# Lengths by products with a column of ones, a k scaled once, 32 decay columns and five sums side by side in a two-layer trunk

## The chip, the core and the metric

The kernel runs on one core of a Trainium2 chip. A core has a matrix engine (TensorE, PE in the profile, with its weight loads shown apart as PEld), a vector engine (VectorE, DVE), an activation engine (ScalarE, ACT), GpSimd (POOL) and SyncE (SP), which issues most of the DMAs. Each engine takes its own queue in order; they wait for each other by semaphores. The metric is the device time of one execution in microseconds, less is better.

## The reference

The reference is a decoder trunk of two layers over 528 positions (16 learned ones and 512 of the input) with 1024 channels, in float32. Layer 0 mixes positions with a chunked gated DeltaNet, layer 1 with a short gated convolution; each mixer is followed by a gated feed-forward with a convolution (2816 channels), and each sub-layer ends in a LayerNorm of 1.41 x + f(x).

The DeltaNet has 8 heads of 128 channels. q, k and v come from a projection, a causal convolution of four taps and a Silu. What the change touches is this:

```python
def l2norm(x):
    return x * lax.rsqrt(jnp.sum(x * x, axis=-1, keepdims=True) + L2_EPS)
...
    q = l2norm(q) * (GDN_HEAD_DIM ** -0.5)
    k = l2norm(k)
    beta = jax.nn.sigmoid(b_raw)
    g = -jnp.exp(a_log) * jax.nn.softplus(a_raw + dt_bias)
...
    decay = jnp.exp(jnp.where(causal, g[..., :, None] - g[..., None, :], -jnp.inf))
    k_beta = k * beta[..., None]
    v_beta = v * beta[..., None]
    m = jnp.where(strict, jnp.einsum("bhnid,bhnjd->bhnij", k_beta, k) * decay, 0.0)
    a_mat = jnp.eye(CHUNK) + m
    u = triangular_solve(a_mat, v_beta);  w = triangular_solve(a_mat, k_beta * exp(g))
```

Here g is the running sum within a chunk; the state then passes through the chunks one after the other.

## The kernel before

Activations lie with channels on the 128 partitions and positions along the free dimension. Every large product is done in three matmuls: an operand is split into a high part (hi, rounded to fp32r by ScalarE) and the rest (lo, by VectorE), and hi*hi, hi*lo and lo*hi are summed in PSUM (lines 286 to 288, `mm_steps`). Weights are loaded in strips of 128 output channels, split by `split` (lines 91 and 92) and used strip by strip; `pump` loads and splits ahead as far as buffers go.

**The recurrence** (lines 345 to 693) takes the 528 positions as five chunks of 106. First come the decay and beta columns: 16 columns of weights, two halves of the positions (tile psba, lines 347 to 350), transposed to positions on partitions (psb), and a series of small operations on 106 x 40 values. `proj` projects k, v and q of a head, in this order, convolves them and applies Silu. `gdn_a` prepares a head: it transposes k and v (pk, pv), forms the products of k with k (pn) and with q (pp), takes lengths from squares of the transposed k and q (lines 473 and 474, 499 to 502), scales the matrix by beta and the lengths (psNb, lines 506 to 510), and inverts it by levels of masked f16 products. `gdn_b` runs the state through the five chunks, `gdn_c` transposes the output back, and `gate` projects z. The matrix of decays of a head (`decay`, tile psE) is made for two heads at a time, both in the PSUM tile ga0; `gdn_a` of even heads uses ga0, of odd heads ga1, one step after another in the same tile.

The generators of three heads are woven (lines 673 to 686), and the projection of a later head follows in program order. The order in which each engine gets its instructions is set by a planner, when the kernel is built: it takes ready instructions by priority, which is program order, and by its own estimates of durations. So projections fill PE between the small steps of the recurrence. On the chip the order is fixed, and an engine that waits holds up all that is planned behind.

**The sub-layers.** `down` multiplies a group of hidden blocks (gh, gl, nk blocks of 128) with the down strips into tiles pd, one sum for each output strip m and half b of the positions, and adds them to h (line 773 for the first group, 775 for later ones). `together` runs several sums side by side, block after block, so that a block that arrives late is needed later. At the start of a group three sums run so. PSUM has six banks for this (tag m) and two others (tag a), which the LayerNorm uses. The out projection is `down` with nk = 8, the first feed-forward uses nk = 4, 6, 6, 6, the short convolution 2 and 6; the last feed-forward has its own function, `down_turned`.

Of the kernel before, what the change touches and what calls it, by code (L numbers as in the profile page):

```python
# [17 lines left out]
P = 128  # L18
# [58 lines left out]
def tile_hybrid_trunk(ctx, tc, xt, par, cst, msk, w_ba, w_qkv, w_z, w_ao, w_bi, w_bo, w_up, w_dn, w_dt, lnr, out):  # L77
# [23 lines left out]
    ba_hi = lnp.tile([P, KD, 16], F32R, name="ba_hi", tag="c", bufs=CB)  # L101
    ba_lo = lnp.tile([P, KD, 16], F32R, name="ba_lo", tag="c", bufs=CB)
# [189 lines left out]
    split(ba_hi, ba_lo, ba_raw)  # L292
# [34 lines left out]
    with ExitStack() as gctx:  # L327
# [17 lines left out]
        ba_sb = gp.tile([16, TP], F32, name="ba_sb", tag="ba_sb")  # L345
        V.memset(ba_sb[:, T:], 0.0)
        psba = gtile("psba", 1).rearrange("p (b c) i -> p b (c i)", b=2)
        for b in range(2):
            mm(psba[:16, b, :HB], (ba_hi, ba_lo), KD, hh, hl, 0, b * HB, HB)
            S.activation(ba_sb[:, b * HB : (b + 1) * HB], psba[:16, b, :HB], AF.Copy)  # L350
        psb = gtile("psb")
        for c in range(NC_):
            TE.transpose(psb[:CH, c, :16], ba_sb[:, c * CH : (c + 1) * CH], ident[:16, :16])
        colb = gp.tile([CH, NH, NC_], F32, name="colb", tag="colb")
        cola = gp.tile([CH, NH, NC_], F32, name="cola", tag="cola")
        S.activation(colb, psb[:CH, :NC_, 0:8].rearrange("p c h -> p h c"), AF.Exp, scale=-1.0)
# [40 lines left out]
        nbeg = cpool.tile([CH, NH, NC_], F32, name="nbeg")  # L397
# [4 lines left out]
        V.tensor_tensor(nbeg, nb, eg, ALU.mult)  # L402

        def decay(hd):
            PT = PTs[hd] = gp.tile([CH, NC_, CH], F32, name=f"PT{hd}", tag="PT", bufs=4)
            ps = outer(gA[:, hd, :], gA_hi[:, hd, :], gA_lo[:, hd, :], tri, f"E{hd}", 0, G)
            S.activation(PT, ps[:CH, :NC_, :CH], AF.Exp)
            G.tensor_tensor(PT, PT, bcm(tri, NC_), ALU.mult)

        def proj(hd, res):  # L410
# [4 lines left out]
            for grp in (1, 2, 0):  # L415
# [15 lines left out]
                S.activation(res[grp][:, :T], acc, AF.Silu)  # L431
            if hd % 2 == 0:
# [23 lines left out]
        def gdn_a(hd, box, qT, kT, vT):  # L456
# [5 lines left out]
            ssk, ssq, rk, nbr, nbe = (small(x) for x in ("ssk", "ssq", "rk", "nbr", "nbe"))  # L462
# [5 lines left out]
            box.update(PT=PT, DT=DT, kd=kd, vb=vb, ssq=ssq, nbe=nbe, rk=rk, qT=qTv, kT=kTv)  # L468

            ps = gtile(f"pk{hd}", ch)  # L470
            for c in R5:
                TE.transpose(ps[:CH, c, :], kTv[:, c, :], ident)
            S.activation(kd, ps[:CH, :NC_, :], AF.Square)
            V.reduce_sum(ssk, kd, axis=AX)
            V.tensor_scalar(ssk, ssk, L2_EPS, None, ALU.add)
            G.tensor_tensor(rk, ssk, halfneg[:CH], ALU.pow)
            V.tensor_tensor(kd, ps[:CH, :NC_, :], bc(ekd[:, hd, :], P), ALU.mult)
# [4 lines left out]
            V.tensor_tensor(vb, ps[:CH, :NC_, :], bc(beta[:, hd, :], P), ALU.mult)  # L482
# [11 lines left out]
            V.tensor_tensor(nbr, rk, nb[:, hd, :], ALU.mult)  # L494
            G.tensor_tensor(NT, NT, bc(rk, CH), ALU.mult)
            yield 900, 1200
            ps = gtile(f"pq{hd}", ch)
            for c in R5:
                TE.transpose(ps[:CH, c, :], qTv[:, c, :], ident)
            sq = gp.tile([CH, NC_, P], F32, name=f"sq{hd}", tag="R", bufs=2)  # L500
            S.activation(sq, ps[:CH, :NC_, :], AF.Square)
            V.reduce_sum(ssq, sq, axis=AX)
            V.tensor_tensor(nbe, nbr, eg[:, hd, :], ALU.mult)
            yield 500, 15000
# [729 lines left out]
```

## Time and profile before

| what | value |
|---|---|
| runs | 1322.82, 1324.2, 1325.62 us (median 1324.2) |
| profiled execution | 1323.19 us, of which the span shown is 1321.2 us |
| granted clock of PE, mean | 0.997 |
| busy: PE, PEld | 1295.1 us (98%), 1244.6 us (94%) |
| busy: DVE, ACT, POOL | 1062.2 us (80%), 739.8 us (56%), 90.1 us (7%) |
| decay columns and recurrence | 0 to about 366 us |
| first feed-forward, its first down projection | from 464 us |
| short convolution, its first down projection | 836 to 849 us |

A matmul's span in the profile is longer than the time that it holds up PE: matmuls overlap, so the time from one start to the next is its cost in a dense stream. An f32 matmul that is not a transpose shows as two instructions. A row of the timeline gives start, length, engine, line, tiles, shapes and count, with the idle time before it and what ended it in brackets. A group row gives count, busy time, mean length in ns, and the idle time before it.

### The profile page before, as it was taken

The page shows a single profiled execution, that of the slowest core. Times are in us where ns is not written, and L with a number is a line of the kernel's source. Part 1 is how long each engine was busy: PE and PEld are TensorE (multiplying, and loading weights), DVE is VectorE, ACT ScalarE, POOL GpSimd, SP SyncE. Part 2 cuts the span into 40 slices and gives each one's busy share as a digit, 9 for nine tenths or more (in the row PEclk, how much of TensorE's full clock was granted, in tenths as well). Part 3 has the DMA queues.
Part 4 walks back from the last instruction along what each step waited for, and adds up shares of the span by engine and source line. Part 5 has one row for each costly group of instructions (what it writes and reads, how often), then busy time and mean ns, then how long its engine had stood idle before and what let it go on. Part 6 is the DMA issues. An engine that isn't in the chain of part 4 may idle for free.

```text
span 1321.2 us, 25891 instructions
## 1 busy us (share of the span) xinstructions
PE 1295.1 (98%) x10545; PEld 1244.6 (94%) x10545; DVE 1062.2 (80%) x1906; ACT 739.8 (56%) x1371; POOL 90.1 (7%) x132
## 2 busy tenths in 40 slices
PE   9999999999999999999999999999999999999997
PEld 8899989999899999999999999999998998998996
DVE  6787878786468888969869789988689795995977
ACT  6567576665345746636537467455476572662660
POOL 0323242211010000000000000000000000000000
PEclk9999999999999999999999999999999999999999
DMA  6211111111261132412422422324033242341231
GB/s 202 79 49 34 47 35 49 49 34 33 65 225 50 52 124 85 140 65 88 152 65 86 139 71 65 107 96 159 18 99 110 74 138 76 97 149 46 97 125 64
DMA packets 36183, 116.81 MB, mean 88 GB/s; under 512 B 4192, under 2 KB 5600, under 8 KB 36064
## 3 DMA queue, kind: packets, MB, share of 16 engines
q1 hardware_dynamic: 35280, 112.77, 27.0%
q0 software_dynamic: 640, 2.12, 0.5%
q8 instruction: 82, 1.34, 0.4%
q14 instruction: 37, 0.30, 0.1%
q10 hardware_dynamic: 144, 0.26, 0.1%
HBM read 113.05 MB, written 2.10 MB: 87 GB/s over the span
## 4 chain that ended last, share of the span: by engine, by line
PE 67%; DVE 5%; ACT 2%; DMA 1%; issue 1%; POOL 0%; DVEq 0%; ACTq 0%; POOLq 0%
PE px L286 6%; PE px L288 6%; PE px L287 6%; PE pd L286 5%; PE pd L287 5%; PE pd L288 5%; PE pz L286 3%; PE pz L287 3%; PE pt L841 3%; PE pt L842 3%; PE pt L843 3%; PE pz L288 3%; PE pu L287 2%; PE pu L288 2%; PE pu L286 2%; PE pq L286 2%
## 5 line engine op out<-in xcount | busy, mean ns | idle before, releaser
L91 ACT ACTIVATE wh<-raw 128x512 fp32r<-128x512 f32 (+3 forms) x309 | 234.7, 766 | 194.3 <-PE pd L287 62.4
L92 DVE TENSOR_TENSOR wl<-raw,wh 128x512 fp32r<-128x512 f32 (+3 forms) x309 | 262.6, 860 | 60.5 <-ACT wh L91 58.6
L286 PE MATMUL pd<-gh,wh 128*128 128x260 f32 (+2 forms) x480 | 135.9, 285 | 2.4 <-ACT gh L91 1.8
L91 ACT ACTIVATE wh<-s 128x512 fp32r<-128x512 f32 x129 | 81.2, 630 | 100.4 <-PE pt L842 45.3
L287 PE MATMUL pd<-gl,wh 128*128 128x260 f32 (+2 forms) x480 | 136.4, 285 | 0.3 <-DVE gl L92 0.3
L288 PE MATMUL pd<-gh,wl 128*128 128x260 f32 (+2 forms) x480 | 135.8, 283 | 0.0
L287 PE MATMUL pu<-hl,wh 128*128 128x258 f32 (+3 forms) x400 | 114.4, 289 | 1.5 <-DVE hl L754 1.4
L286 PE MATMUL pu<-hh,wh 128*128 128x258 f32 (+3 forms) x400 | 113.2, 288 | 0.7 <-ACT wh L91 0.7
L288 PE MATMUL pu<-hh,wl 128*128 128x258 f32 (+3 forms) x400 | 113.4, 288 | 0.5 <-DVE wl L92 0.5
L286 PE MATMUL ps<-hh,wh 128*128 128x264 f32 x384 | 113.5, 296 | 0.3 <-ACT acc L425 0.3
L288 PE MATMUL ps<-hh,wl 128*128 128x264 f32 x384 | 113.7, 297 | 0.0
L287 PE MATMUL ps<-hl,wh 128*128 128x264 f32 x384 | 113.2, 295 | 0.0
L92 DVE TENSOR_TENSOR wl<-s,wh 128x512 fp32r<-128x512 f32 x129 | 88.5, 686 | 12.7 <-ACT wh L91 10.6
L286 PE MATMUL px<-sumh,wh 128*128 128x258 f32 (+1 forms) x344 | 97.6, 284 | 0.0
L288 PE MATMUL px<-sumh,wl 128*128 128x258 f32 (+1 forms) x344 | 97.5, 283 | 0.0
L287 PE MATMUL px<-suml,wh 128*128 128x258 f32 (+1 forms) x344 | 97.3, 283 | 0.0
L286 PE MATMUL px<-hh,wh 128*128 128x258 f32 (+1 forms) x344 | 97.2, 283 | 0.0
L288 PE MATMUL px<-hh,wl 128*128 128x258 f32 (+1 forms) x344 | 96.9, 282 | 0.0
L287 PE MATMUL px<-hl,wh 128*128 128x258 f32 (+1 forms) x344 | 96.9, 282 | 0.0
L286 PEld LDWEIGHTS pd<-gh,wh 128*128 128x128 f32 x480 | 90.5, 189 | 3.1 <-ACT gh L91 2.0
L287 PEld LDWEIGHTS pd<-gl,wh 128*128 128x128 f32 x480 | 91.4, 191 | 0.7 <-DVE gl L92 0.5
L288 PEld LDWEIGHTS pd<-gh,wl 128*128 128x128 f32 x480 | 91.4, 191 | 0.0
(319 smaller groups left out, 4069.0 us busy)
## 6 DMA issues: line engine op xcount, KB each, us to landing
raw<-in_w_up_dram SPq DMA_DIRECT2D x88, 512.0 KB, 3.7
raw<-in_w_bi_dram SPq DMA_DIRECT2D x24, 512.0 KB, 3.7
raw<-in_w_qkv_dram SPq DMA_DIRECT2D x23, 512.0 KB, 3.6
raw<-in_w_dt_dram SPq DMA_DIRECT2D x22, 512.0 KB, 4.4
raw<-in_w_dn_dram SPq DMA_DIRECT2D x24, 384.0 KB, 3.5
raw<-in_w_z_dram SPq DMA_DIRECT2D x8, 512.0 KB, 3.6
raw<-in_w_ao_dram SPq DMA_DIRECT2D x8, 512.0 KB, 3.6
raw<-in_w_bo_dram SPq DMA_DIRECT2D x8, 384.0 KB, 3.5
```

The source lines that it names most:

```text
L91: S.activation(hi, src, AF.Copy)
L92: V.tensor_tensor(lo, src, hi.bitcast(F32), ALU.subtract)
L286: TE.matmul(ps, hi[:, k, :], r_h, start=start and k == 0, stop=False, **kw)
L287: TE.matmul(ps, hi[:, k, :], r_l, start=False, stop=False, **kw)
L288: TE.matmul(ps, lo[:, k, :], r_h, start=False, stop=stop and k == nk - 1, **kw)
L841: TE.matmul(ps, gh[:, k, ts_], w_h, start=k == 0, stop=False)
L842: TE.matmul(ps, gl[:, k, ts_], w_h, start=False, stop=False)
L843: TE.matmul(ps, gh[:, k, ts_], w_l, start=False, stop=k == nk - 1)
```

## The change

- **Decay columns**: hi and lo weights stand side by side in one tile of 32 columns, multiplied with hh and with hl (32 matmuls in place of 48, lo*lo included); the two halves are added after the transposes. In place of beta its square root is made, by a power on GpSimd.
- **Lengths**: `proj` squares k and q on ScalarE as they are; `gdn_a` begins with ten products of these squares with one column of ones (pss), which give the sums of squares of both. The squares of the transposed k and q, their two reductions and the transposes of q (pq) are gone.
- **k scaled once** by sqrt(beta) / length after its transposes (kn), and transposed back over the old k (pkt). So the products of k come out scaled; the psNb products and the scaling around them are gone, and the matrix is masked with ntri on GpSimd. v is scaled with sqrt(beta), and the scale of vn in `gdn_b` is gone.
- **Second decay in the other bank**: the decay of odd heads uses ga1.
- **Five sums**: `down` begins a first group with five sums side by side instead of three, outside of the final group with the last two in the spare banks. With nk = 2 all sums run one after another, each fourth in a spare bank.

```diff
-            mm(psba[:16, b, :HB], (ba_hi, ba_lo), KD, hh, hl, 0, b * HB, HB)
+            for k in range(KD):
+                for x in (hh, hl):
+                    TE.matmul(psba[:32, b, :HB], ba_w[:, k, :], x[:, k, b * HB : (b + 1) * HB],
+                              start=k == 0 and x is hh, stop=k == KD - 1 and x is hl)
...
+        S.activation(bas, psb[:CH, :NC_, 16:32], AF.Copy)
+        V.tensor_tensor(bas, bas, psb[:CH, :NC_, 0:16], ALU.add)
...
-        V.reciprocal(beta, colb)
+        G.tensor_tensor(sbeta, colb, hn, ALU.pow)
+        V.tensor_tensor(ntri, ident[:CH, :CH], tri, ALU.subtract)
...
-            ps = outer(gA[:, hd, :], gA_hi[:, hd, :], gA_lo[:, hd, :], tri, f"E{hd}", 0, G)
+            ps = outer(gA[:, hd, :], gA_hi[:, hd, :], gA_lo[:, hd, :], tri, f"E{hd}", hd % 2, G)
...
                 S.activation(res[grp][:, :T], acc, AF.Silu)
+                if grp < 2:
+                    sq = gp.tile([P, TP], F32, name=f"sq{hd}_{grp}", tag="zs", bufs=2)
+                    S.activation(sq, res[grp], AF.Square)
+                    sqs.setdefault(hd, []).append(sq)
...
-            ps = gtile(f"pk{hd}", ch)
-            for c in R5:
-                TE.transpose(ps[:CH, c, :], kTv[:, c, :], ident)
-            S.activation(kd, ps[:CH, :NC_, :], AF.Square)
-            V.reduce_sum(ssk, kd, axis=AX)
-            V.tensor_scalar(ssk, ssk, L2_EPS, None, ALU.add)
+            sqk, sqq = (qv(x) for x in sqs.pop(hd))
+            ps = gtile(f"pss{hd}", ch)
+            for g_, x in enumerate((sqk, sqq)):
+                for c in R5:
+                    TE.matmul(ps[:CH, 0, g_ * NC_ + c : g_ * NC_ + c + 1], x[:, c, :], one1[:, :1], start=True, stop=True)
+            V.tensor_scalar(ss.rearrange("p g c -> p (g c)"), ps[:CH, 0, : 2 * NC_], L2_EPS, None, ALU.add)
             G.tensor_tensor(rk, ssk, halfneg[:CH], ALU.pow)
-            V.tensor_tensor(kd, ps[:CH, :NC_, :], bc(ekd[:, hd, :], P), ALU.mult)
+            V.tensor_tensor(rk, rk, sbeta[:, hd, :], ALU.mult)
...
-            V.tensor_tensor(vb, ps[:CH, :NC_, :], bc(beta[:, hd, :], P), ALU.mult)
+            V.tensor_tensor(vb, ps[:CH, :NC_, :], bc(sbeta[:, hd, :], P), ALU.mult)
+            ps = gtile(f"pk{hd}", ch)
+            for c in R5:
+                TE.transpose(ps[:CH, c, :], kTv[:, c, :], ident)
+            kn = gp.tile([CH, NC_, P], F32, name=f"kn{hd}", tag="R", bufs=2)
+            V.tensor_tensor(kn, ps[:CH, :NC_, :], bc(rk, P), ALU.mult)
+            V.tensor_tensor(kd, kn, bc(ekd[:, hd, :], P), ALU.mult)
+            ps = gtile(f"pkt{hd}", ch)
+            for c in R5:
+                TE.transpose(ps[:, c, :CH], kn[:, c, :], ident[:CH, :CH])
+            S.activation(kTv, ps[:, :NC_, :CH], AF.Copy)
...
-            V.tensor_tensor(nbr, rk, nb[:, hd, :], ALU.mult)
-            G.tensor_tensor(NT, NT, bc(rk, CH), ALU.mult)
-            ps = gtile(f"pq{hd}", ch)
-            for c in R5:
-                TE.transpose(ps[:CH, c, :], qTv[:, c, :], ident)
-            sq = gp.tile([CH, NC_, P], F32, name=f"sq{hd}", tag="R", bufs=2)
-            S.activation(sq, ps[:CH, :NC_, :], AF.Square)
-            V.reduce_sum(ssq, sq, axis=AX)
-            V.tensor_tensor(nbe, nbr, eg[:, hd, :], ALU.mult)
-            bn = gp.tile([CH, NC_, CH], F32, name=f"bn{hd}", tag="B", bufs=2)
-            V.tensor_tensor(bn, bcm(ident[:CH, :CH], NC_), bc(nbr, CH), ALU.mult)
-            ps = gtile(f"psNb{hd}", ch)
-            TE.matmul(ps[:CH, 0:4, :CH], strict, bn[:, 0:4, :], start=True, stop=True)
-            TE.matmul(ps[:CH, 4, :CH], strict, bn[:, 4, :], start=True, stop=True)
-            V.tensor_tensor(NT, NT, ps[:CH, :NC_, :CH], ALU.mult)
+            G.tensor_tensor(NT, NT, bcm(ntri, NC_), ALU.mult)
...
-                S.activation(vn[:, c, :], sa[:CH, 1, :], AF.Copy, scale=rk[:, c : c + 1])
+                S.activation(vn[:, c, :], sa[:CH, 1, :], AF.Copy)
...
-        def go(m, b):
+        def go(m, b, spare=False):
...
+        if not final and nk < 3:
+            for x in range(2 * KD):
+                together(go(x // 2, x % 2, x % 4 == 3))
+            return
         if not final:
-            together(go(0, 0), go(0, 1), go(1, 0))
-            together(go(1, 1))
-            for m in range(2, KD):
-                together(go(m, 0))
-                together(go(m, 1))
+            n = 5 if first else 3
+            together(*[go(x // 2, x % 2, x > 2) for x in range(n)])
+            for x in range(n, 2 * KD):
+                together(go(x // 2, x % 2))
             return
         warm()
         keep = KD - (HOLD6 if nk == 6 else HOLD8)
-        together(go(0, 0), go(0, 1), go(1, 0))
-        together(go(1, 1)) if keep > 1 else None
-        for m in range(2, KD):
-            together(go(m, 0))
+        n = 5 if first else 3
+        together(*[go(x // 2, x % 2) for x in range(n)])
+        for m in range(1 if n == 3 else 2, KD):
+            if 2 * m >= n:
+                together(go(m, 0))
             if m < keep:
                 together(go(m, 1))
```

More of the change, by code (lines that the diff above doesn't have):

```diff
@@ L100, in tile_hybrid_trunk @@
     ba_raw = lnp.tile([P, KD, 16], F32, name="ba_raw", tag="c", bufs=CB)
-    ba_hi = lnp.tile([P, KD, 16], F32R, name="ba_hi", tag="c", bufs=CB)
-    ba_lo = lnp.tile([P, KD, 16], F32R, name="ba_lo", tag="c", bufs=CB)
+    ba_w = lnp.tile([P, KD, 32], F32R, name="ba_w", tag="c", bufs=CB)
     onesm = cpool.tile([P, P], F32, name="onesm")
@@ L290, in mm_steps @@
                 yield
-    split(ba_hi, ba_lo, ba_raw)
+    split(ba_w[:, :, :16], ba_w[:, :, 16:], ba_raw)
     split(hh[:, 0, :], hl[:, 0, :], h[:, 0, :])
@@ L342, in gbank @@
             return pg.tile([P, 4, P], F32, name=name, tag=tag, bufs=1)
-        ba_sb = gp.tile([16, TP], F32, name="ba_sb", tag="ba_sb")
+        ba_sb = gp.tile([32, TP], F32, name="ba_sb", tag="ba_sb")
         V.memset(ba_sb[:, T:], 0.0)
@@ L396, in tile_hybrid_trunk @@
         egl = cpool.tile([P, NH, NC_], F32, name="egl")
-        nbeg = cpool.tile([CH, NH, NC_], F32, name="nbeg")
+        neg = cpool.tile([CH, NH, NC_], F32, name="neg")
         fl = lambda t_: t_.rearrange("p h c -> p (h c)")
@@ L461, in gdn_a @@
             full = lambda nm, bufs=2, dt=F32: gp.tile([CH, NC_, CH], dt, name=f"{nm}{hd}", tag=nm, bufs=bufs)
-            ssk, ssq, rk, nbr, nbe = (small(x) for x in ("ssk", "ssq", "rk", "nbr", "nbe"))
+            rk = small("rk")
+            ss = gp.tile([CH, 2, NC_], F32, name=f"ss{hd}", tag="ss", bufs=3)
+            ssk, ssq = ss[:, 0, :], ss[:, 1, :]
             NT, DT = full("NT"), full("DT", 3)
@@ L573, in gdn_b @@
         def gdn_b(hd, box):
-            PT, DT, kd, vb, ssq, nbe, rk, qTv, kTv = (
-                box[x] for x in ("PT", "DT", "kd", "vb", "ssq", "nbe", "rk", "qT", "kT"))
+            PT, DT, kd, vb, ssq, qTv, kTv = (box[x] for x in ("PT", "DT", "kd", "vb", "ssq", "qT", "kT"))
             vn = gp.tile([CH, NC_, P], F32, name=f"vn{hd}", tag="vn")
@@ L586, in gdn_b @@
                     TE.matmul(sb[:CH, c - 1, :], qTv[:, c, :], St, start=True, stop=True)
[L587 removed]
+                    V.scalar_tensor_tensor(rr, sa[:CH, 0, :], neg[:, hd, c : c + 1], vb[:, c, :], ALU.mult, ALU.add)
                     r_ = rr
@@ L613, in gdn_b @@
             V.reduce_sum(sso, vn, axis=AX)
-            V.tensor_scalar(ssq, ssq, L2_EPS, RMS_EPS * P * P, ALU.add, ALU.mult)
+            V.tensor_scalar(ssq, ssq, RMS_EPS * P * P, None, ALU.mult)
             V.tensor_tensor(sso, sso, ssq, ALU.add)
@@ L710, in tile_hybrid_trunk, with bank @@
     V.tensor_scalar(ntap, par_sb[:, OFF_BCONV:OFF_LN], -1.0, None, ALU.mult)
-    def bank(name):
-        return pm.tile([P, 512], F32, name=name, tag="m")
+    def bank(name, spare=False):
+        return (pa if spare else pm).tile([P, 512], F32, name=name, tag="a" if spare else "m")
     def together(*its):
@@ L766, in go @@
                 sts[m] = get()
-            ps = bank(f"pd{idx}_{m}_{b}_{state['use']}")[:, : c1 - c0]
+            ps = bank(f"pd{idx}_{m}_{b}_{state['use']}", spare)[:, : c1 - c0]
             yield from mm_steps(ps, sts[m], nk, xh, xl, 0, c0 - xoff, c1 - c0, every=1)
```

31 lines of the change are left out of this document (14 added, 17 removed).

## The prediction

> **What bounds the kernel now.** I read the page's totals first, then the busy time of each engine by stretch, then what TensorE (PE) waited for, then single stretches in order of time.
>
> ```profile
> span 1321.2 us, 25891 instructions
> PE 1295.1 (98%) x10545; PEld 1244.6 (94%) x10545; DVE 1062.2 (80%) x1906; ACT 739.8 (56%) x1371; POOL 90.1 (7%) x132
> ...
> 17.00:366.00 349.00, 339.30 (x3195) 321.01 (x3194) 269.22 (x468) 212.11 (x399) 83.57 (x103) 1.00 0.17 51
> ...
> 467.00:469.20 2.20, 0.39 (x5) 0.18 (x3) 2.20 (x5) 1.54 (x3) 0.00 (x0) 1.00 0.49 201
> 469.20:474.00 4.80, 4.80 (x27) 4.80 (x28) 3.92 (x7) 2.06 (x4) 0.00 (x0) 0.64 0.00 0
> ...
> 835.00:849.00 14.00, 13.41 (x111) 13.05 (x110) 13.47 (x30) 4.66 (x8) 0.00 (x0) 1.00 0.18 49
> ```
>
> The columns of the stretches are length, then PE, PEld, DVE, ACT and POOL busy time, granted clock, DMA share and GB/s. PE is busy for 98% of the span, so time is matmul work plus PE's idle time. In the recurrence (17 to 366 us) it is idle for 349.0 - 339.3 = 9.7 us, with DVE at 269 of 349 us. A change there is worth the PE work that it adds or removes, and what it does to those 9.7 us.
>
> ```profile
> PE pd L286 <- ACT gh L91: 1.8, 1, 1.8
> PE pot L628 <- DVE oS L618: 1.7, 2, 1.2
> PE pv L481 <- DVE kd L477: 1.6, 1, 1.6
> PE psE L451 <- ACT PT L407: 1.6, 2, 0.8
> ...
> PE pq L499 <- DVE PT L493: 0.9, 3, 0.4
> ...
> PE pd L286 <- DVE h L773: 0.6, 1, 0.6
> ...
> PE pn L486 <- DVE vb L482: 0.5, 1, 0.5
> ```
>
> Each row is a wait of PE: total us, times, longest. None is large, and no one wait carries the kernel.
>
> **The change, part by part.**
>
> *PE work of the recurrence.* The projections' matmuls fill PE between the recurrence's small groups, so each small group costs its start-to-start time.
>
> ```profile
> 34.54 0.35 PE L391 MATMUL psc<-gA,cst_sb 106*106 106x40 f32 x2 [0.25 <-DVE gA L379]
> 34.72 0.36 PE L392 MATMUL psc<-gA,cst_sb 106*106 106x40 f32 x2
> 34.91 0.39 PE L393 MATMUL psc<-gA,one 106*128 106x40 f32 x2
> ...
> 144.82 0.76 PE L499 MATMUL pq<-cst_sb,qkv 128*106 128x128 f32 x5 [0.18 <-DVE PT L493]
> 145.44 0.67 PE L628 MATMUL pot<-cst_sb,oS 106*128 106x106 f32 x5
> 145.95 0.39 PE L590 MATMUL sa<-rr,DT 106*106 106x128 f32 x2
> ...
> 146.37 0.96 PE L508 MATMUL psNb<-bn,cst_sb 106*106 106x424 f32 x2
> 147.17 0.41 PE L543 MATMUL pt<-ident,D 106*106 106x106 f16 x5
> 147.41 0.39 PE L509 MATMUL psNb<-bn,cst_sb 106*106 106x106 f32 x2
> 147.64 0.41 PE L594 MATMUL sa<-vn,kd 106*128 106x128 f32 x2
> ```
>
> Removed per head: the transposes of q (pq), 145.44 - 144.82 = 0.62 us, and the two psNb products, (147.17 - 146.37) + (147.64 - 147.41) = 1.03 us; 1.65 us together. Added: five transposes of the scaled k back (pkt). They have pot's shape, so 145.95 - 145.44 = 0.51 us. Then ten products with the column of ones (pss). The trace has none with one moving column. The nearest are psc's: f32, 106 stationary columns, 40 moving columns, issued as two passes each, 34.72 - 34.54 = 0.18 and 34.91 - 34.72 = 0.19 us a product. The lower bound is the f16 group pt, five one-pass products of 106 columns in 147.41 - 147.17 = 0.24 us, 48 ns a pass, so 0.10 us a product. I take 0.185, since psc shares type, passes and stationary width, and its 40 moving columns already cost as much as wide ones; ten cost 1.85 us (lower bound 0.96). So PE gains 0.51 + 1.85 - 1.65 = 0.7 us a head, **+5.7 us** over eight heads (-1.4 by the lower bound).
>
> The Trainium skill has two rules here, both on its page "TensorE: Matmul & The Clock Gate". Section "LDWEIGHTS (loading the stationary operand)" has a weight load take its columns over 1.2 GHz, whatever moves: 88 ns for 106 columns, with which psc's 90 to 95 ns a pass agrees. Section "Wait — 56ns, not 53.3ns?" puts the floor between small matmuls near 25 ns; by it alone 20 passes would cost an estimated 0.5 us a head and the step would turn into a gain of some 5 us.
>
> *The decay columns.* Three matmuls for each of 8 row blocks and 2 halves become two of 32 columns: 48 - 32 = 16 fewer.
>
> ```profile
> 17.08 0.28 PE L288 MATMUL psba<-hh,ba_lo 128*16 128x264 f32 x1
> 17.20 0.28 PE L286 MATMUL psba<-hh,ba_hi 128*16 128x264 f32 x1
> 17.32 0.28 PE L287 MATMUL psba<-hl,ba_hi 128*16 128x264 f32 x1
> ```
>
> They start 0.12 us apart, and moving columns, not output columns, set this: **-1.9 us**, since PE is dense there (bound 0, if the start waits for data anyway). The added Copy, add, power and mask before the recurrence are off PE's path: projections cover them.
>
> *VectorE and ScalarE.*
>
> ```profile
> L502 DVE TENSOR_REDUCE ssq<-sq 106x5 f32<-106x640 f32 x8 | 6.6, 820 | 5.4 <-ACT sq L501 5.4
> L477 DVE TENSOR_TENSOR kd<-pk,ekd 106x640 f32<-106x640 f32 x8 | 6.5, 816 | 0.0
> ...
> L474 DVE TENSOR_REDUCE ssk<-kd 106x5 f32<-106x640 f32 x8 | 6.5, 815 | 0.2 <-ACT kd L473 0.2
> ...
> L506 DVE TENSOR_TENSOR bn<-cst_sb,nbr 106x530 f32<-106x530 f32 x8 | 6.1, 760 | 0.0
> ...
> L510 DVE TENSOR_TENSOR NT<-NT,psNb 106x530 f32<-106x530 f32 x8 | 5.6, 706 | 2.1 <-PE psNb L509 2.0
> ```
>
> DVE loses two reductions, bn and the product with psNb, 0.82 + 0.815 + 0.76 + 0.706 = 3.1 us a head, and gains the scaled k, by kd's row 0.82 us: some 18 us less in the stage. ScalarE swaps two squares and gains one copy, a half microsecond a head. Both are hidden under PE; the worth is in waits. The replaced waits are pv's, psE's, pq's and pn's: 1.6 + 1.6 + 0.9 + 0.5 = 4.6 us. psE's goes because the second decay no longer needs the bank that the first one's Exp is still reading. New waits come: pkt needs the scaled k from DVE, pn needs ScalarE's copy, each behind whatever stands ahead in those queues, and PE's queue stands behind them. A decay's bank is still read by its Exp when the next step wants it. Bounds: all 4.6 come back, or DVE's relief takes most of the 9.7 (8 saved). I take **-3.5 us**, one wait of about 1 us returning. On POOL the mask product takes the place of one with the scale, no change.
>
> *Five sums.* In the first feed-forward down projection PE runs three sums side by side until it needs the fourth gh block:
>
> ```profile
> 462.30 1.28 ACT L91 ACTIVATE wh<-raw 128x512 fp32r<-128x512 f32 x2 [2.24 <-DMA raw<-in_w_dn_dram]
> ...
> 463.98 0.28 PE L286 MATMUL pd<-gh,wh 128*128 128x260 f32 x1
> ...
> 467.08 0.28 PE L288 MATMUL pd<-gh,wl 128*128 128x260 f32 x1
> 469.18 0.74 PE L286 MATMUL pd<-gh,wh 128*128 128x260 f32 x4 [1.81 <-ACT gh L91]
> ...
> 472.09 0.41 PE L287 MATMUL pd<-gl,wh 128*128 128x256 f32 x1
> 472.31 0.41 PE L288 MATMUL pd<-gh,wl 128*128 128x256 f32 x1
> ```
>
> Three sums give 27 matmuls before the wait (463.98 to 467.2); five give 45, 5.4 us at 0.12, to 469.4, past the gh that ends the wait at 469.18. The third strip's weights are there: the last down strip's wh is written at 463.6, before the sums begin. That takes the 1.8 us. Right behind the wait matmuls start 0.22 apart instead of 0.12; the granted clock of that stretch is 0.64 over 4.8 us, a loss of at most 0.36 x 4.8 = 1.7 us; I count 1.5, some 16 matmuls at 0.09 us each. All other stretches quoted here were granted 1.00, so I tie it to the idle time: **-3.3 us** (bounds 0 and -3.5). The same page, section "HAM oscillation — how this bites in real kernels", re-throttles only after idle gaps above about 3.4 us; this row shows it after 1.8, so the rule and the row differ, and by the rule the 1.5 us might stay. In the short convolution's first down projection (nk 2) each fourth sum goes to one of the two spare banks. PE is idle 0.6 us there for an eviction (h L773) and DVE is busy for 13.47 of 14 us; two more banks hold 1.4 us of PE work: **-0.6 us** (0 to -0.8; DVE may hand it back later). In the out projection the stall comes before the first product, so five sums give nothing.
>
> **Sum.** 5.7 - 1.9 - 3.5 - 3.3 - 0.6 = -3.6 us. The profiled execution took 1323.19 us (span plus 2.0); less 3.6 is 1319.6. The median of the runs shown is 1324.2, 1.0 above it, so I set the time midway, **1320.0 us**.
>
> **Rivals.**
>
> *A, the forecast*: 1320, own range 1317 to 1323. Chance 0.43.
>
> *B, VectorE's relief is worth more.* If 8 of the 9.7 idle us go instead of 3.5: 4.5 us less, 1315.5. For it: three of the four replaced waits name DVE or its results. Against: pot's wait (1.7) and others have nothing to do with it. Chance 0.17.
>
> *C, five sums don't do what they say.* The third strip or DVE's order makes PE wait as before and the half clock stays: 3.3 comes back, 1323.3, no change. For it: DVE is busy all 2.2 us of the stall, so gh's place in its queue, not the sums' number, set it. Against: 18 more matmuls are simply enough. Chance 0.18.
>
> *D, slower: the first step now needs q.* Before, a head's chain began with k alone; now the ten products need squares of k and of q, and q's strip is projected last.
>
> ```profile
> 132.51 0.60 PE L472 MATMUL pk<-cst_sb,qkv 128*106 128x128 f32 x4
> ...
> 137.22 0.65 ACT L431 ACTIVATE qkv<-acc 128x528 f32<-128x528 f32 x1 [1.16 <-DVE ssk L475]
> ```
>
> Head 3's pk starts at 132.5 but its q comes from the Silu at 137.2 to 137.9; the square follows behind ScalarE's queue. Projections can fill that, if the planned order puts them ahead. Where pss stands at the head of PE's queue too early, PE waits as it did once for pv, 1.65 us; eight such waits, 13 us, less the 3.6 gained and with B's side gone: about 1329. It decides from 0.5 us a head on (3.6 / 8). Against: the order is planned with the dependence known. Chance 0.17.
>
> *E, the products with ones cost the lower bound*: 5.7 becomes -1.4, 7.1 less, 1313. Against: psc. Chance 0.05.
>
> **How the numbers follow.** About 0.2% (2.6 us) is what a measurement of this kernel can tell from no change. A's centre lies 3.6 to 4.2 below the runs, so some two thirds of A is faster (0.28) and the rest same (0.15); B and E are faster (0.22); C is same (0.16) or just faster (0.02); D is same in 0.04 and slower in 0.13. Faster 0.52, same 0.35, slower 0.13. The range 1314 to 1327 leaves out E's far half and D's upper half.
>
> **What would show it.** Right: between 17 and 366 us PE's matmul count rises, the ten pss products start about 0.09 us a pass, the stage's idle time falls below 7 us, psE's wait is gone, and the stage ends within 1.5 us of 366. No half clock near 470 us, and no wait of pd for gh. Wrong: pss passes at 50 ns (E); waits of PE for the squares of q or for kn (D); a pd wait for gh or its weights that is still there (C). If the time is off by over 6 us, the sum of waits, not matmul work, was misjudged.

## The result, and the profile after

The changed kernel took 1344.84 us (median of 4 runs, 1341.52 to 1346.53), the kernel before 1324.74 us beside it: ratio 1.0154, 95% interval 1.0140 to 1.0168. It is 20 us slower, where 4 us faster was forecast. The profiled execution after took 1341.52 us, 18.3 more than the one of before.

Totals of the changed kernel's page:

```profile
span 1339.7 us, 26041 instructions
PE 1306.3 (98%) x10657; PEld 1256.9 (94%) x10657; DVE 1045.8 (78%) x1873; ACT 733.0 (55%) x1373; POOL 98.5 (7%) x133
```

Busy time by stretch, changed kernel (columns as before):

```profile
100.00:110.00 10.00, 8.85 (x47) 8.55 (x48) 0.90 (x1) 4.52 (x6) 6.88 (x9) 0.66 0.19 52
262.00:270.00 8.00, 7.93 (x55) 7.73 (x56) 4.68 (x5) 4.32 (x7) 2.93 (x3) 0.79 0.20 68
17.00:366.00 349.00, 330.08 (x3131) 313.12 (x3130) 244.13 (x417) 197.86 (x385) 90.70 (x103) 0.99 0.16 48
488.00:497.00 9.00, 9.00 (x76) 8.81 (x75) 8.38 (x16) 5.72 (x10) 0.00 (x0) 1.00 0.39 141
```

TensorE has 112 matmul instructions more, as the edits count (160 pss and 40 pkt more; 40 pq, 32 psNb and 16 psba fewer). Yet within 17 to 366 us PE idles 18.9 us, not 9.7, and two places run at a granted clock of 0.66 and 0.79; that is (1 - 0.66) x 10 + (1 - 0.79) x 8 = 5.1 us of lost clock.

Where the 18 us arise is read from the first product after the recurrence (tile pd); timeline of before, then of after:

```profile
369.13 0.39 PE L286 MATMUL pd<-hh,wh 128*128 128x262 f32 x1 [0.59 <-ACT zs L642]
...
490.43 0.28 PE L286 MATMUL px<-hh,wh 128*128 128x260 f32 x1
```

```profile
392.96 0.39 PE L286 MATMUL pd<-hh,wh 128*128 128x262 f32 x1 [0.59 <-ACT zs L650]
...
510.88 0.28 PE L286 MATMUL px<-hh,wh 128*128 128x260 f32 x1
```

The recurrence ends 23.8 us later. From there to the first px (the end of the first feed-forward) it is 117.9 us, not 121.3, and to the end of the span 946.8, not 952.1: the rest of the kernel gained 5.3. So the whole loss lies before 393 us. The stage up to this product, before and after:

```profile
17.00:369.13 352.13, 341.84 (x3215) 323.34 (x3213) 271.62 (x472) 215.24 (x406) 84.96 (x106) 1.00 0.17 52
17.00:392.96 375.96, 355.18 (x3332) 337.13 (x3330) 256.58 (x438) 208.75 (x408) 93.25 (x107) 0.99 0.16 49
```

VectorE is relieved by 15.0 us, near the 18 that were forecast. But PE idles 20.8 us, not 10.3. These 10.5 us, the 5.1 us of lost clock and 6.4 us of added matmul work (measured below) make 22.0 of the 23.8 us; the rest is not accounted for.

What PE waited for there, changed kernel (total, times, longest):

```profile
PE psE L461 <- POOL blE L457: 3.9, 5, 1.3
PE p L533 <- DVE PT L518: 3.4, 6, 0.9
PE psE L460 <- POOL bhE L456: 2.8, 4, 1.5
PE pot L636 <- DVE oS L626: 1.7, 2, 1.3
PE pk L498 <- DVE vb L494: 1.2, 2, 0.9
PE p L540 <- ACT DT L553: 1.2, 1, 1.2
```

psE's wait did not go; it went from 1.6 to 6.7 us and changed its releaser from ScalarE's Exp to GpSimd's operands. A new wait of 3.4 us is p's, the first inversion product. Groups of before, then of after, show why p waits:

```profile
L495 POOL TENSOR_TENSOR NT<-NT,rk 106x530 f32<-106x530 f32 x8 | 11.8, 1475 | 29.1 <-DVE NT L487 26.2 <-DVE nbe L503 2.9
L511 ACT ACTIVATE T<-NT 106x530 f16<-106x530 f32 x8 | 5.1, 639 | 0.4 <-DVE NT L510 0.4
L512 DVE TENSOR_SCALAR N<-NT 106x530 f16<-106x530 f32 x8 | 3.5, 435 | 0.1
```

```profile
L486 PE MATMUL pss<-one,sq 128*106 128x1 f32 x160 | 17.3, 233 | 0.0
L519 POOL TENSOR_TENSOR NT<-NT,ntri 106x530 f32<-106x530 f32 x8 | 12.0, 1501 | 51.4 <-DVE NT L512 51.4
L457 POOL TENSOR_TENSOR blE<-cst_sb,gA_lo 106x424 fp32r<-106x424 f32 x8 | 9.5, 1189 | 0.0
L456 POOL TENSOR_TENSOR bhE<-cst_sb,gA_hi 106x424 fp32r<-106x424 f32 x8 | 9.1, 1141 | 7.6 <-PE psE L460 7.6
L520 ACT ACTIVATE T<-NT 106x530 f16<-106x530 f32 x8 | 5.2, 647 | 8.3 <-POOL NT L519 5.9 <-POOL cb L425 2.4
L521 DVE TENSOR_SCALAR N<-NT 106x530 f16<-106x530 f32 x8 | 3.5, 440 | 9.7 <-POOL NT L519 7.4 <-POOL cb L425 2.3
```

GpSimd's product on NT costs the same, 1.48 and 1.50 us. But before, the psNb products and a VectorE product stood between it and the f16 copies T and N, which waited 0.4 and 0.1 us in all. Now the copies follow it directly and wait 8.3 and 9.7 us. While VectorE stands at N, the product PT is queued behind it, and the tile that PT reads is the one that p wants.

At the decays, PE's timeline of after near 100 us, with GpSimd's row from the same time:

```profile
98.42 1.92 POOL L456 TENSOR_TENSOR bhE<-cst_sb,gA_hi 106x424 fp32r<-106x424 f32 x1 [5.81 <-PE psE L460]
...
100.39 0.44 PE L460 MATMUL psE<-bhE,strict_r 106*106 106x424 f32 x1 [1.46 <-POOL bhE L456]
101.71 0.44 PE L461 MATMUL psE<-blE,strict_r 106*106 106x424 f32 x1 [0.75 <-POOL blE L457]
...
102.32 0.42 PE L287 MATMUL ps<-hl,wh 128*128 128x264 f32 x1
102.53 0.42 PE L288 MATMUL ps<-hh,wl 128*128 128x264 f32 x1
...
109.31 0.28 PE L287 MATMUL ps<-hl,wh 128*128 128x264 f32 x1
109.43 0.29 PE L288 MATMUL ps<-hh,wl 128*128 128x264 f32 x1
```

With its own bank the second decay is planned right behind the first. GpSimd could not begin its operand until the first decay's product freed the buffer (it idled 5.81 us for that), and then takes 1.92 and 1.35 us for the two operands. PE idles 1.46 and 0.75 us, and then the projections start 0.21 us apart, not 0.12, until 109.2 us.

### The profile page after: what moved, and what is told of

It is laid out like the page before. It is cut to its first block, busy times and chain, and to the rows that moved or that the text cites. A ratio compares the mean times of both kernels' runs of the same rounds, so it can differ in the third digit from the quotient of the medians.

```text
span 1339.7 us, 26041 instructions
## 1 busy us (share of the span) xinstructions
PE 1306.3 (98%) x10657; PEld 1256.9 (94%) x10657; DVE 1045.8 (78%) x1873; ACT 733.0 (55%) x1373; POOL 98.5 (7%) x133
## 4 chain that ended last, share of the span: by engine, by line
PE 86%; DVE 6%; POOL 3%; ACT 2%; issue 2%; DMA 1%; SPq 0%; DVEq 0%; POOLq 0%; ACTq 0%
PE px L286 6%; PE px L288 6%; PE px L287 6%; PE pd L287 5%; PE pd L286 5%; PE pd L288 5%; PE pu L287 3%; PE pu L288 3%; PE pu L286 3%; PE pz L286 3%; PE pt L855 3%; PE pt L856 3%; PE pt L857 3%; PE pz L287 3%; PE pz L288 3%; PE ps L288 3%
## 6 DMA issues: line engine op xcount, KB each, us to landing
raw<-in_w_dn_dram SPq DMA_DIRECT2D x24, 384.0 KB, 3.6
raw<-in_w_bo_dram SPq DMA_DIRECT2D x8, 384.0 KB, 3.5
```

## The experiments

Ratios are to the kernel before, run beside each version. "pd" is the start of the first product after the recurrence (before: 369.1 us; after: 393.0). It comes from one execution, and its start varies by itself (the last psba product begins between 16.0 and 19.3 us in these traces), so the ratios decide.

### Parts of the change added to the kernel before

**Five sums alone** (`bank` and `down` as changed).

> The kernel before with the five sums alone (new starts of the down projections and the two spare banks). Theory: the wait for gh near 467 us (1.8 us), the half clock behind it (1.5 us) and the wait for an eviction near 840 us (0.6 to 1.0 us) go: 3.5 to 5.5 us faster, 0.996 to 0.9973 of before. Rival: VectorE's order, not the number of sums, set the wait, and the spare banks only move it: 0 to 1.5 us faster, 0.999 to 1.0.

Measured: 1321.72 us, ratio 0.9986 (0.9977 to 0.9995). Its timeline has the first px at

```profile
487.40 0.28 PE L286 MATMUL px<-hh,wh 128*128 128x260 f32 x1
```

and its waits of PE have a new one:

```profile
PE px L286 <- ACT sc L1026: 1.2, 1, 1.2
```

px comes 3.0 us earlier than in the kernel before (490.43), with the same start of pd: the wait for gh and its half clock are gone, as forecast. The new wait, 1.2 us for a scale, is in the short convolution, so 1.9 us are left at the end, between the two expectations.

**Five sums and 32 columns** (old beta, old recurrence).

> The kernel before with five sums and the 32 decay columns, the recurrence and its beta as before. Theory: 16 matmuls at 0.12 us fewer in a dense stretch, 1.9 us less than with the five sums alone: 5.5 to 7.5 us faster than before, 0.9943 to 0.9958. Rival: the start waits for x and its splitting, so the columns give nothing, or the new order of the start costs as much: as with five sums alone, 0.996 to 0.9975.

Measured: 1319.38 us, ratio 0.9968 (0.9956 to 0.9981); pd at 366.2. The columns are worth 2.4 us by the ratios and 2.9 by pd, as forecast; that the ratio still lies in the rival's range comes from the five sums, which gave less than expected. This part of the change beats both kernels.

**The same without the spare banks of the short convolution** (nk = 2 as before).

```diff
-        if not final and nk < 3:
-            for x in range(2 * KD):
-                together(go(x // 2, x % 2, x % 4 == 3))
-            return
```

> The kernel before with five sums and the 32 decay columns (1319.4 us, ratio 0.9968) and one edit: the short convolution's first down projection (nk 2) goes without the spare banks, as in the kernel before. Theory 1, what the spare banks win there is given back in the pairs that follow, where px waits 1.2 us for a scale: no difference, 1318.5 to 1320.5 us, ratio 0.9962 to 0.9977. Rival, the spare banks cost the 1.2 us: 1317.5 to 1318.5 us, ratio 0.995 to 0.9962.

Measured: 1318.02 us, ratio 0.9955 (0.9943 to 0.9968), the fastest kernel of the study. The interval overlaps that of the version with spare banks, so they win nothing that can be measured and may cost a little. The wait of px is gone; one of 1.5 us for an eviction (pd for h) has come.

**The second decay's bank alone.**

```diff
-            ps = outer(gA[:, hd, :], ..., f"E{hd}", 0, G)
+            ps = outer(gA[:, hd, :], ..., f"E{hd}", hd % 2, G)
```

> The kernel before with one edit: the second decay of a pair goes to ga1. Theory 1 (the bank is the fault by itself): PE's wait moves from the Exp (1.6 us) to GpSimd's operands, 4 to 7 us, with half clock behind the longest: 4 to 10 us slower, 1.003 to 1.0075 of before. Theory 2 (the bank does harm only together with the new steps of a head, or none at all): the 1.6 us wait goes and nothing comes, 0.9985 to 1.001.

Measured: 1326.28 us, ratio 1.0023 (1.0014 to 1.0033); pd at 374.2. Waits of PE in this version:

```profile
PE psE L452 <- POOL blE L448: 1.8, 3, 1.3
...
PE psE L451 <- POOL bhE L447: 1.6, 3, 0.6
```

Its stretch behind two of them:

```profile
98.00:101.50 3.50, 3.50 (x19) 3.49 (x18) 1.29 (x2) 0.73 (x2) 3.50 (x4) 0.51 0.25 98
```

So the edit turns the 1.6 us wait for the Exp into 3.4 us for GpSimd, with 1.7 us of lost clock behind it, and costs 3 us by the ratios. PE's idle time from 17 us to pd is hardly longer (10.5 us, before 10.3), so other waits shrank, and these rows alone do not add up to the 3 us.

### Parts taken out of the changed kernel

**One bank** (both decays in ga0 again).

> The changed kernel with one edit undone: both decays of a pair go to PSUM tile ga0 again. Theory 1 (the bank): in the changed kernel PE stands at the second decay's products while GpSimd still makes their operands (psE waits for POOL 6.7 us in all, against 1.6 us for the Exp before), and two of these stands are followed by half clock for 6.8 and 3.4 us, some 5 us lost. Then this kernel is 8 to 11 us faster than the changed one, 1.0065 to 1.009 of the kernel before, has no psE wait above 2 us in all and no half clock in the recurrence. Theory 2 (the longer start of a head: squares of q, scaled k, mask on GpSimd): the wait only moves to the next step of the tile, gain 0 to 3 us, 1.013 to 1.0155 of before.

Measured: 1335.13 us, ratio 1.0087 (1.0074 to 1.0099); pd at 384.0. psE waits 1.0 us for GpSimd instead of 6.7, and PE's idle time from 17 us to pd falls from 20.8 to 14.0 us. That is 8.9 us by the ratios. But 10.2 us at half clock remain, against the expectation, at other places. The first row is the stretch just ahead of the first half clock; PE is not idle in it:

```profile
102.31:105.72 3.41, 3.41 (x33) 3.08 (x31) 0.90 (x3) 3.41 (x9) 3.41 (x5) 1.00 0.31 124
105.72:109.13 3.41, 3.20 (x18) 3.16 (x18) 2.03 (x6) 1.01 (x2) 1.18 (x2) 0.50 0.00 0
262.73:269.56 6.83, 6.83 (x39) 6.83 (x39) 4.09 (x8) 1.26 (x3) 1.17 (x1) 0.50 0.12 19
```

**Four operand buffers, bank kept** (tag B with `bufs=4`).

> The changed kernel (1344.8 us, ratio 1.0154) with one edit: four buffers in place of two for GpSimd's operands of the decays (tag B). Theory 1, the second decay in its own bank comes to TensorE before GpSimd has made its operands, and GpSimd cannot make them before the first decay's products free the two buffers (it idles 7.6 us for them): with four buffers they are made earlier, the 6.7 us wait of psE falls below 2 us and the time to that of one bank: 1333 to 1337 us, ratio 1.007 to 1.010. Rival, GpSimd's own pace (1.1, 1.2 and 0.8 us one after the other for each head) decides, not the buffers: 1341 to 1346 us, ratio 1.013 to 1.0165.

Measured: 1338.37 us, ratio 1.0104 (1.0088 to 1.0119): of the bank's 8.9 us it takes away 6.6. psE's wait falls from 6.7 to 3.2 us, where below 2 was expected; 2.4 of them are one wait at the first pair, where GpSimd begins only when gA is there; half clock follows that one, as the stretch shows:

```profile
38.00:48.50 10.50, 9.90 (x46) 9.73 (x47) 2.94 (x2) 3.81 (x6) 8.94 (x10) 0.51 0.17 50
```

**Second decay's operands on VectorE, bank kept.**

```diff
-            ps = outer(..., hd % 2, G)
+            ps = outer(..., hd % 2, V if hd % 2 else G)
```

> The changed kernel with one edit: the operands of the second decay of each pair are made on VectorE in place of GpSimd. Theory 1, GpSimd's pace makes psE wait: the 6.7 us of psE's wait for GpSimd falls below 2 us, the half clock behind it goes, VectorE takes on some 2 us a pair that it has room for: 1333 to 1338 us, ratio 1.007 to 1.0105. Rival, VectorE's queue is as late as GpSimd (what stands ahead there waits for TensorE itself) and psE waits for VectorE: 1341 to 1347 us, ratio 1.013 to 1.017.

Measured: 1336.32 us, ratio 1.0090 (1.0076 to 1.0104), as with one bank; no wait of psE is left among those listed. Both mends say the same: with the operands on time the bank gains nothing over one bank; its cost is that GpSimd's operands come late.

**Mask on VectorE** (with one bank).

```diff
-            G.tensor_tensor(NT, NT, bcm(ntri, NC_), ALU.mult)
+            V.tensor_tensor(NT, NT, bcm(ntri, NC_), ALU.mult)
```

> The changed kernel with both decays in one bank (1335.1 us, ratio 1.0087) and one more edit: the strip's strict lower mask (eight operations of 1.50 us) is on VectorE in place of GpSimd. Theory 1, late operands: VectorE no longer stands behind the GpSimd mask, so the wait of the p products for the PT product (3.4 us) goes, and part of the half clock after it: 1330 to 1332.5 us, ratio 1.0050 to 1.0068. Rival, the wait is only passed on to the next operation of the same chain (the mask costs VectorE eight times some 0.7 us): 1334 to 1336 us, ratio 1.0080 to 1.0096.

Measured: 1330.56 us, ratio 1.0049 (1.0033 to 1.0065); pd at 378.1. Groups of this version:

```profile
L519 DVE TENSOR_TENSOR NT<-NT,ntri 106x530 f32<-106x530 f32 x8 | 5.6, 705 | 0.1
L520 ACT ACTIVATE T<-NT 106x530 f16<-106x530 f32 x8 | 5.1, 641 | 4.0 <-DVE NT L519 4.0
```

Its stage by stretch:

```profile
17.00:366.00 349.00, 337.48 (x3251) 322.17 (x3250) 254.91 (x438) 201.51 (x396) 81.46 (x96) 1.00 0.17 50
```

The product takes 0.705 us there, p's wait for PT is gone, and the clock stays at 1.00. The mask on GpSimd cost 5.0 us by the ratios. Not all of that is the wait for it: between the two profiles PE's idle time from 17 us to pd falls by 1.9 us (14.0 to 12.1), and 5.1 us of lost clock go. Over all runs the granted clock has a mean of 0.995 with the mask on GpSimd and 0.997 here, some 2 us; how the 5.0 us divide stays open.

**Both mended, bank kept** (four buffers and the mask on VectorE).

> The changed kernel, second decay in its own bank kept, with four buffers for the decays' operands (ratio 1.0104 alone) and the mask on VectorE (worth 0.0038 with one bank). Theory 1, the two late operands add up and the other bank gains nothing: 1331.5 to 1335 us, ratio 1.005 to 1.008. Rival, the other bank does gain the wait for the first decay's Exp once its operands are early: 1326 to 1330 us, ratio 1.001 to 1.0045.

Measured: 1334.95 us, ratio 1.0079 (1.0065 to 1.0093): the other bank is still 4 us worse than one bank with this mask. The mask gains 3.3 us here. The 2.4 us wait at the first pair stays, with 6.8 us of half clock behind it.

**The fastest kernel with the bank and four buffers.**

> The kernel before with the 32 columns and five sums in the long groups (ratio 0.9955), the second decay in the other bank and four buffers for the decays' operands. Theory 1, the bank edit gains nothing even with more buffers, GpSimd's operands are late for the earlier place: 1318.5 to 1322 us, ratio 0.9955 to 0.998. Rival, the wait for the first decay's Exp (1.6 us before) is gained: 1315.5 to 1317 us, ratio 0.9935 to 0.9945.

Measured: 1319.42 us, ratio 0.9962 (0.9948 to 0.9975): no gain from the bank there either.

### The products and the scaling

**Two products instead of ten** (one bank; each with the squares of block 0 and five columns of ones; the squares of the other four blocks are left out).

```diff
-                for c in R5:
-                    TE.matmul(ps[:CH, 0, g_ * NC_ + c : g_ * NC_ + c + 1], x[:, c, :], one1[:, :1], ...)
+                TE.matmul(ps[:CH, 0, g_ * NC_ : (g_ + 1) * NC_], x[:, 0, :], one1[:, :NC_], ...)
```

> The changed kernel with both decays in one bank, and the lengths of a head made by two products with five columns of ones (the squares of block 0 of k and of q stand for all five blocks) in place of ten products with one column: eight products and eight weight loads a head are left out, the outputs are not the reference's. Theory 1, the products count in full on TensorE: 64 products of 0.186 us are 11.9 us less than 1335.1, so 1322 to 1325 us, ratio 0.999 to 1.0015. Rival, the first step waits for the squares and TensorE would only wait longer: 1330 to 1335 us, ratio 1.005 to 1.009.

Measured: 1322.26 us, ratio 0.9984 (0.9974 to 0.9993), 13.6 us less than with ten by the ratios. **The same with the mask on VectorE:**

> The changed kernel with one bank, the mask on VectorE (1330.6 us, ratio 1.0049) and two products with five columns of ones a head in place of ten with one (the squares of block 0 stand for all blocks, the outputs are not the reference's). Theory 1, what is left above the kernel with five sums and 32 columns (1319.4 us) is the products' own work, 64 products of 0.186 us or 11.9 us: 1317 to 1320.5 us, ratio 0.9942 to 0.9968. Rival, TensorE waits longer for VectorE where the products go, since the chain of a head is now the limit: 1322 to 1327 us, ratio 0.998 to 1.0018.

Measured: 1319.76 us, ratio 0.9964 (0.9950 to 0.9978), 11.3 us less than with ten. The eight products' work, 11.9 us by their measured passes, comes back within the intervals. Some waits grow in its place: PE's idle time from 17 us to pd rises by 1.7 and 2.0 us, and with the mask on GpSimd a wait of 2.7 us (sa for St) has half clock behind it.

**Lengths alone** (five sums, 32 columns, the ten products; k not scaled, psNb kept).

> The kernel before with five sums, the 32 decay columns (1319.4 us together) and, of the recurrence, the lengths alone: squares taken in the strips, ten products with a column of ones, no transposes of q, no row sums on VectorE; k is not scaled, the product psNb and its factors stay. Theory 1, TensorE's work decides: 15.1 us of products less 4.5 us of transposes of q are 10.6 us more, less up to 3 us of VectorE's relief: 1327 to 1331 us, ratio 1.0025 to 1.0055. Rival, the 15.7 us of the recurrence come from scaling k (longer chain, GpSimd mask): 1319 to 1324 us, ratio 0.996 to 1.0005.

Measured: 1337.83 us, ratio 1.0105 (1.0088 to 1.0123); pd at 390.3. That is 18 us above the version without them, more than the 10.6 of PE work, and outside both expectations. In its profile (the slowest of its runs, 1341.2 us) PE idles 5.2 us more from 17 us to pd, and 17.1 us at half clock cost 8.5 us.

**Scaling alone** (five sums, 32 columns, kn and pkt, mask on GpSimd; lengths by squares of the transposed k and q).

> The kernel before with five sums, the 32 decay columns (1319.4 us together) and, of the recurrence, the scaling alone: k scaled once by sqrt(beta)/length and turned back (pkt), GpSimd mask, no product psNb; the lengths stay row sums of squares of the transposed k and q. Theory 1, TensorE's work decides: 3.6 us of pkt less 7.8 us of psNb are 4.2 us less: 1314 to 1317 us, ratio 0.993 to 0.9955. Rival, the chain from the sums over the power and the two scalings to pkt, and the mask on GpSimd, are late: 1322 to 1330 us, ratio 0.999 to 1.005.

Measured: 1336.41 us, ratio 1.0091 (1.0075 to 1.0106), though PE has 4 us less work. The largest waits are pv for kn (4.0 us, once) and py for DT on VectorE (3.8). From 17 us to pd PE idles 24.7 us, 16.0 more than without the scaling, and 1.7 us of clock are lost. The expectations put it lower, both of them. With its mask on GpSimd it is to be compared with both halves on one bank, 1.0087: no difference. So each half alone costs as much as both together or more. The scaling alone loses by idle time, which fits its longer chain (sums on VectorE, power, two scalings, pkt, before the matrix can begin), and the lengths alone lose by work and half clock (below). Which step of the chain holds PE up, no run separates.

**q ahead of v** (one bank, mask on VectorE).

```diff
-            for grp in (1, 2, 0):
+            for grp in (1, 0, 2):
```

> The changed kernel with both decays in one bank and the mask on VectorE (1330.6 us, ratio 1.0049) and one edit: the strips of a head come in the order k, q, v in place of k, v, q, weights included. Theory D of the prediction, the first step of a head stands late because it needs the squares of q: with q earlier the ten products can start some 6 us earlier a head, and 3 to 6 us of TensorE's idle time in the recurrence go: 1325 to 1328 us, ratio 1.0005 to 1.003. Theory 1, the products' own work and the chain through VectorE decide, q is early enough: 1329.5 to 1332 us, ratio 1.004 to 1.006.

Measured: 1336.76 us, ratio 1.0094 (1.0080 to 1.0107): 6 us slower, outside both expectations. That TensorE stands and waits for q isn't what costs. The stretches of this version in the recurrence, at clock 1.00 in the version with v first:

```profile
17.00:60.00 43.00, 41.18 (x329) 39.34 (x328) 30.57 (x63) 26.80 (x51) 21.06 (x19) 0.96 0.28 87
60.00:140.00 80.00, 77.84 (x756) 75.03 (x755) 57.76 (x90) 48.69 (x91) 16.73 (x25) 0.96 0.14 41
140.00:220.00 80.00, 77.95 (x744) 74.98 (x743) 60.65 (x100) 48.97 (x93) 17.90 (x29) 0.96 0.15 41
```

**What lowers the clock.** 0.04 x 203 = 8 us of clock are lost there, without a wait above 1.0 us. A stretch at half clock in the version with lengths alone:

```profile
189.50:196.50 7.00, 6.74 (x39) 6.61 (x39) 4.36 (x11) 2.16 (x4) 1.30 (x2) 0.51 0.01 2
```

PE's timeline of that version just before it:

```profile
187.56 1.09 PE L485 MATMUL pss<-one,sq 128*106 128x1 f32 x10 [0.21 <-ACT PT L412]
188.51 0.37 PE L286 MATMUL ps<-hl,wh 128*128 128x264 f32 x1
188.71 0.28 PE L287 MATMUL ps<-hh,wl 128*128 128x264 f32 x1
188.84 1.18 PE L485 MATMUL pss<-one,sq 128*106 128x1 f32 x10
```

Two groups of products with one moving column stand right ahead of the half clock, and little idle time. To tell the two apart, the products were given 100 moving columns of ones, in three versions (the shifted plan of the other engines goes with it):

```diff
-                    TE.matmul(ps[:CH, 0, g_ * NC_ + c : g_ * NC_ + c + 1], x[:, c, :], one1[:, :1], ...)
+                    TE.matmul(pw[:CH, g_ * 512 + c * 100 : g_ * 512 + (c + 1) * 100], x[:, c, :], one1[:, :100], ...)
```

> The version with the lengths alone (1337.8 us, ratio 1.0105) with each of the ten products moving 100 columns of ones in place of one: the same sums a hundred times over, the same weight loads, one more small VectorE operation a head; the order planned for the engines shifts with it. Theory, a group of products with one moving column counts as idle time for TensorE's clock: the half clock that followed such groups there near 46, 76, 189 and 271 us does not come, its 8 us of lost clock come back, the passes get 0.008 us longer (1.3 us in all): 1328 to 1333 us, ratio 1.003 to 1.007. Rival, the idle time beside the groups lowers the clock: half clock stays in some places, 1336 to 1341 us, ratio 1.009 to 1.013.

> The changed kernel with both decays in one bank (1335.1 us, ratio 1.0087) with 100 moving columns of ones in each of the ten products. Theory, products with one moving column count as idle time for the clock: no half clock behind the products (it followed them at 105.5 and 262.5 us), 5 us back and 1.3 us more for the passes: 1329.5 to 1333 us, ratio 1.004 to 1.007. Rival, the idle time beside them lowers the clock: 1334 to 1338 us, ratio 1.008 to 1.011.

> The version with one bank, the mask on VectorE and q ahead of v (1336.8 us, ratio 1.0094) with 100 moving columns of ones in each of the ten products. Theory, products with one moving column count as idle time for the clock: no half clock behind the products (it followed them at 43, 108 and 186.5 us), 8 us back and 1.3 us more for the passes: 1328 to 1332 us, ratio 1.003 to 1.006. Rival, the idle time beside them lowers the clock: 1335.5 to 1340 us, ratio 1.008 to 1.012.

Measured: lengths alone 1333.44 us, ratio 1.0071 (1.0056 to 1.0087), was 1.0105; one bank 1337.64 us, 1.0095 (1.0081 to 1.0110), was 1.0087; q ahead of v 1330.27 us, 1.0039 (1.0026 to 1.0053), was 1.0094. Lengths alone and q ahead of v came out as the theory had it; one bank came out in the rival's range. The stage in the three, in this order:

```profile
17.00:366.00 349.00, 336.84 (x3204) 319.61 (x3203) 255.75 (x452) 200.47 (x385) 79.03 (x102) 1.00 0.16 48
```

```profile
17.00:366.00 349.00, 334.08 (x3195) 316.60 (x3192) 248.19 (x431) 197.30 (x390) 90.08 (x103) 1.00 0.16 48
```

```profile
17.00:366.00 349.00, 335.79 (x3239) 321.00 (x3239) 254.87 (x446) 202.94 (x396) 77.61 (x96) 1.00 0.17 49
```

The clock is 1.00 in all three, with 12.2, 14.9 and 13.2 us of idle time and waits of up to 1.8 us. Two gained 4.5 and 7.3 us. One bank did not: its stage idles more (14.9 us, before it 12.2), and the gain of the clock went there. What a fuller clock is worth depends on the waits that the new plan has.

The traces tell the two causes apart further. Half clock comes in them in stretches of 3.41, 6.83 or 10.24 us, and full clock between two of them lasts a multiple of 3.41 us too (45 times that, from 109.13 to 262.73 us of the changed kernel). So I compare the 3.41 us ahead of each half clock. Between 17 and 1300 us the 20 traces have 18 half clocks. Ahead of nine, PE was idle by the profile for 1.6 to 2.75 us of the 3.41. Ahead of the other nine it was idle for 0 to 0.9 us, and exactly these nine hold 10 to 20 passes with one moving column, 0.087 us each. Now take idle time and such passes together, in all 7471 stretches of 3.41 us at full clock: 17 have more than 1.72 us, and half clock followed 14 of these; 11 have 1.60 to 1.72 us, and it followed 4; all others have less, and it followed none. So in these traces the passes with one moving column count for the clock as if PE were idle, and about half of such a stretch is enough, whichever of the two fills it. The version with one bank and the mask on VectorE keeps its clock with the same ten products because no stretch of it gets there (at most 0.70 us idle and 0.87 us of passes). Ahead of the two half clocks of the changed kernel stands idle time alone, psE's waits: 2.2 and 1.7 us.

## Why the prediction was wrong

Step by step, by ratios of versions that differ in one part (0.001 is 1.3 us): five sums -1.9 us, columns -2.4, the recurrence with one bank and the mask on VectorE +10.7, the mask on GpSimd +5.0, the other bank +8.9. They add up to the whole result because they are differences along one chain of versions; each is known to within 2 to 3 us, and depends on the order (the mask is worth 3.3 us, not 5.0, with the bank kept and four buffers).

- **PE work of the recurrence, +5.7: right.** The trace after has ten pss passes from 39.04 to 39.91 us, 0.087 us each (0.0925 forecast), and rival E, with passes of 50 ns, falls by it:

```profile
39.04 1.01 PE L486 MATMUL pss<-one,sq 128*106 128x1 f32 x10
39.91 0.37 PE L286 MATMUL ps<-hh,wh 128*128 128x264 f32 x1
```

  Summed from start to start over the stage, pss took 15.1 us and pkt 3.6, and pq and psNb had taken 4.5 and 7.8: +6.4. Leaving eight of ten out gave back 11.3 and 13.6 us. The Trainium skill's rule on loading the stationary operand ("TensorE: Matmul & The Clock Gate", section "LDWEIGHTS (loading the stationary operand)"), 88 ns for 106 columns, agrees with the 87 ns.
- **Decay columns, -1.9: right** (-2.4; pd 2.9 us earlier). The power on GpSimd took 6.8 us, once, off the path: psc, PE's next step there, starts at 31.8 us, before at 34.5.
- **Waits, -3.5: wrong, and the step that failed.** PE's idle time from 17 us to pd did not shrink by 3.5 us, it grew by 10.5, and 5.1 us of lost clock came with it. Three of its sentences fail. "psE's goes because the second decay no longer needs the bank": the bank's wait hid a second one for GpSimd's operands, and the earlier place exposed it (6.7 us of waiting, half clock behind). "On POOL the mask product takes the place of one with the scale, no change": its length is unchanged, but what stood between it and its readers was removed. "DVE's relief" came (271.6 to 256.6 us busy up to pd), and PE's idle time rose all the same: PE waits for single results of VectorE, GpSimd and ScalarE, and when these come is not set by VectorE's total; rival B falls by the same rows. The half clock that follows was not in the sum at all. The prediction had named this as the step to doubt if the time was off by over 6 us.
- **Five sums, -3.3: right in place and size** (px 3.0 us earlier, of which 1.9 are left at the end; no wait of pd for gh after, clock 1.00 at 488 to 497 us). Rival C falls. **Short convolution, -0.6: not found**; the version without it is 1.4 us faster at overlapping intervals.
- **Rival D had the right side, by another mechanism.** In the changed kernel pss has no idle time ahead of it (0.0 in its row above), and taking q ahead of v did not gain. With 100 columns that order gives 1.0039, and 1.0049 is the time of v first with one column: no difference beyond the intervals. Its price in the prediction was added wrongly: the forecast of 1320 already holds the 3.6 us gained, so 13 us more make 1333, not 1329.
- **The range**, 1314 to 1327, left out at its upper end that a wait may grow past the one it replaces, and that lost clock comes with it.

Open: of the 10.7 us that the recurrence's edits cost at best, 6.4 are PE's work. pd is 12.0 us later, of which 2.5 lie in the start, before the recurrence. From 17 us to pd PE idles 3.4 us more (12.1, not 8.7), in waits for VectorE's results of at most 2.2 us in all each (pot for oS, pt for D, sa for St). No run separates these. That the plan shifts with each edit, and some of the idle time with it, is argued from the runs with 100 columns, not shown for each version.

## What to carry to other kernels

When an edit frees a resource that an instruction waited for, look up who would release it next: the operand's maker, its buffers, its queue. And when a step between a slow engine's product and its readers is removed, the product's latency becomes visible though its duration is unchanged. Edits that come as one package are best timed in parts: here the 32 columns and the five sums of the long groups were worth keeping (1318 us, 0.45% faster than before), and the rest hid them.

## What was not expected of the hardware

- The granted clock falls not only after idle time. Passes with one moving column, 0.087 us each and no gap between them, count as well: with one bank half clock began at 105.72 us, right behind 3.41 us without any idle time that held 20 of them. With 100 moving columns no half clock came in three versions between 17 and 1300 us. The Trainium skill ("TensorE: Matmul & The Clock Gate", section "What's actually happening") ties the clock to how busy the array has been of late and lowers it after an idle window of about 3.4 us. The half clocks here, 3.41, 6.83 and 10.24 us long, fit such a window and its multiples. The idle time differs: gaps of 1.46 and 0.75 us, 2.2 us within 3.41, were enough to start one in the changed kernel.
- GpSimd's power is slow for its size: 6.78 us for 106 x 40 values, where the operand product of 106 x 424 values took between 0.89 and 1.92 us.
